# Moving split weights by 64 bytes in SBUF: channel-major pieces at one offset, three placements in the wide products

## The chip, the core and the metric

The kernel runs on one core of a Trainium2 chip. The metric is the device time of one launch in microseconds (us); the time quoted is the median over several runs. A profile is one execution recorded instruction by instruction.

## What is computed

A two-layer decoder trunk on 256 rows of width 2048. Layer 0 is a Mamba-2 mixer, layer 1 an attention over keys and values that are projected from the output of layer 0. Nearly all the arithmetic is in the big projections:

```
proj = h @ in_w                      # 2048 -> 10304: z, x, B, C, dt
y    = chunked_scan(conv(x), ...) * silu(z);  y = group_rms_norm(y) @ out_w   # 4096 -> 2048
x    = layer_norm(alpha*x + (1+gate)*y)
k, v = split(x @ kv_w)               # 2048 -> 2 x 3072
q, z = split(h @ b_in_w)             # 2048 -> 3072 + 1024
o    = merge(attention(q, k, v)) * silu(z);   x = layer_norm(alpha*x + (1+gate)*(o @ b_out_w))
```

where h is x scaled and shifted by two vectors that are matrix products of a condition vector c (scale, shift and gate of each layer). Inputs, weights and output are float32.

## The kernel before

**Split products.** A float32 operand is written as a high half (rounded to the matmul type fp32r) and a low half (what is left), and a product is the sum of three: high x high, high x low, low x high. Weights come from memory in pieces of 128 x 1024 float32 (512 KB). `load_piece` issues the transfer on SP's queue into one of six `raw` tiles; `split` (L96) makes the halves: ScalarE writes `whi` (L99), VectorE writes `wlo` (L101). `whi` and `wlo` are tiles of 128 x 1024 with four buffers each, in the pool `wp`. Beside them, for the activations, stands the long-lived tile `actT`.

**Four forms of product.** They differ in which operand is loaded into the array (stationary, one weight load for each matmul) and which streams through it (moving):

- `cm_piece` (L150 to L152), channel-major: a 128 x 128 block of `whi` or `wlo` is stationary, 256 columns of activations stream. Three matmuls for each block, 24 for each piece.
- `cm_wide` (L181, L184), channel-major: a block of `whi` is stationary for 512 moving columns (the high and low activations beside each other), then a block of `wlo` for 256 columns (the high activations alone). A group of four matmuls (two L181, two L184) does one step of 128 inputs; a product has 16 groups. It serves the xs projections of layer 0 from the third group on ("xs"), the keys ("k"), the queries ("q") and the gate of layer 1 ("z").
- `tm_mults` (L212 to L214), token-major: a 128 x 128 block of activations is stationary and 512 columns of `whi` or `wlo` stream. It serves z of layer 0, the output projections and the values.
- `dt_piece` (L612 to L614): like `cm_piece`, for the 64 dt columns.

**Order of the work.** The first stage (to about 165 us) has a hand-written list `order` of weight pieces between the 32 transfers of 1 MB that make scale and shift of layer 0; each h step waits for two of those. Then follow, in program order, the groups of the scan with one `bc`, `xs` and `z` product each and the scan's own work between them (to about 490 us), the output projection (to 768 us), keys (to 902 us) and values (to 968 us), queries with attention and the gate of layer 1 (to 1183 us), and the last projection with the layer norm. `upcoming` is a list of the pieces that come next, so that the last piece of one product already splits the first of the next (`begin_next`, `first_or`).

**Places in SBUF.** Pools are laid one behind the other in the order in which they are opened: `cons` (constants; among them `cc`, a 32-column tile `pad` that nothing uses, and `ones`, 128 x 128), `wp`, `act` (`actT`), `sm`, `slots`, and the stage pools. `cc` holds the identity, a triangle, and a mask whose last 128 columns are all ones. `ones` is set by VectorE at the start and used by `warm` (matmuls that do nothing but raise the clock, L435) and by one cumulative sum (L698).

Of the kernel before, what the change touches and what calls it, by code (L numbers as in the profile page):

```python
# [9 lines left out]
F32 = mybir.dt.float32  # L10
# [8 lines left out]
P = 128  # L19
# [30 lines left out]
def trunk(ctx, tc, xT, x, c, par, cst, bias, lnrow, ada, wdt, win, wxs, wout, wk, wv, wbin, wbout, out):  # L50
# [20 lines left out]
    nc.scalar.dma_start(crow, c)  # L71
    cc = cons.tile([P, NCONST], F32, name="cc")

    cons.tile([P, 32], F32, name="pad")

    def pv(name):
        a, b = OFF[name]
        return prm[:, a - NB:b - NB]
# [1 line left out]
    ident = cc[:, CI:CI + 128]  # L80
    tri = cc[:, CT:CT + 128]
    cbmask = cc[:, CM:CM + 384]
    ones = cons.tile([P, P], F32, name="ones")
    V.memset(ones, 1.0)


    def rows(t, b):

# [4 lines left out]
        nc.sync.dma_start(raw, src)  # L93
        return raw

    def split(raw, into=None, after=None):  # L96

        hi, lo = into or [wp.tile([P, 1024], F32R, name=n, bufs=4) for n in ("whi", "wlo")]
        copied.append(S.activation(hi, raw, AF.Copy))  # L99
        with tc.issue_after(after) if after is not None else ExitStack():  # L100
            latest.append(V.tensor_tensor(lo, raw, hi.bitcast(F32), op=ALU.subtract))  # L101
        return hi.rearrange("p (k n) -> p k n", k=2), lo.rearrange("p (k n) -> p k n", k=2)
# [7 lines left out]
            with tc.issue_after(copied[-1].ins), tc.issue_after(latest[-1].ins):  # L110
                owed.pop(0)()

    def first_or(src, q):

        return ready.pop() if ready else split(load_piece(src[q]))

    def begin_next():

        if upcoming:
            src, q = upcoming.pop(0)  # L120
            ready.append(split(load_piece(src[q])))

    def behind_next():

# [15 lines left out]
    def cm_piece(src, q, ps, ahi, alo, k0=0, k1=KT, w=None, after=None, ks=(0, 1)):  # L140


        hi, lo = w or split(load_piece(src[q]), after=after)
        for k in ks:
            kt = 2 * q + k
            for n in range(4):
                o = ps[n // 2][:, n % 2, :]
                c_ = slice(n * P, n * P + P)
                first = kt == k0 and n % 2 == 0
                T.matmul(o, hi[:, k, c_], ahi[:, kt, :], start=first, stop=False, skip_group_check=True)  # L150
                T.matmul(o, hi[:, k, c_], alo[:, kt, :], start=False, stop=False, skip_group_check=True)  # L151
                T.matmul(o, lo[:, k, c_], ahi[:, kt, :], start=False, stop=kt == k1 - 1, skip_group_check=True)  # L152
# [4 lines left out]
    def cm_quad(src, ahi, alo, rate=(0, 1), k0=0):  # L157
        ps = acc_pair()
        for q in range(k0 // 2, KT // 2):
            w = first_or(src, q)  # L160
            if q == KT // 2 - 1:
                begin_next()
            cm_piece(src, q, ps, ahi, alo, k0=k0, w=w)
            background(*rate)
        return ps

    def cm_wide(src, dst, rate=(0, 1), moving=None, later=False):

        both, high = moving or (lambda kt: xp[:, kt], lambda kt: xhi[:, kt, :])
        ps = acc_pair()  # L170
        for q in range(KT // 4):
            w = first_or(src, q)
            if q == 1:
                settle()
            if q == KT // 4 - 1:
                begin_next()
            hi, lo = (t.rearrange("p k n -> p (k n)").rearrange("p (k n) -> p k n", k=4) for t in w)
            for k in range(4):
                kt = 4 * q + k
                for n in range(2):  # L180
                    T.matmul(ps[n], hi[:, k, n * P:n * P + P], both(kt), start=kt == 0, stop=False,  # L181
                             skip_group_check=True)
                for n in range(2):
                    T.matmul(ps[n][:, 0, :], lo[:, k, n * P:n * P + P], high(kt), start=False, stop=kt == KT - 1,  # L184
                             skip_group_check=True)
            background(*rate)
        def put():
            for n in range(2):
                S.activation(dst[:, n, :], ps[n][:, 1, :], AF.Copy)
                V.tensor_tensor(dst[:, n, :], ps[n][:, 0, :], dst[:, n, :], op=ALU.add)  # L190

        if later:
            owed.append(put)
        else:
            with behind_next():
                put()
# [137 lines left out]
    with ExitStack() as cA:  # L334
# [15 lines left out]
        with ExitStack() as cS:  # L350
# [38 lines left out]
            def xs_wide(g):  # L389

                xs[g] = pxs.tile([P, 4, L], F32, name="xs")
                for w in range(2):
                    t = xs[g][:, 2 * w:2 * w + 2, :]
                    cm_wide(wxs[2 * g - 4 + w], t, rate=R, moving=(lambda kt: hp[:, :, kt, :], hh_))
                    for n in range(2):
                        conv(t[:, n, :], 4 * g + 2 * w + n, t[:, n, :])

# [31 lines left out]
            with ExitStack() as c0:  # L429
                pe = c0.enter_context(tc.tile_pool(name="pe", bufs=2))  # L430

                def warm(n, at, after=None):
                    for _ in range(n):
                        with tc.issue_after(after.ins) if after is not None else ExitStack():
                            after = T.matmul(at[:, 0, :P], ones, ones, start=True, stop=True)  # L435
                    return after

                at = mm.tile([P, 2, L], F32, name="acc")
# [111 lines left out]

                def high_half(i):

                    halves[i] = [wp.tile([P, 1024], F32R, name=n, bufs=4) for n in ("whi", "wlo")]
                    copied.append(S.activation(halves[i][0][:, 512:], pieces[i][:, 512:], AF.Copy))

                def low_half(i):
# [47 lines left out]
                def dt_piece(q, raw):  # L604

                    if q == 0:
                        pss["dt"] = mm.tile([P, 2, L], F32, name="acc")[:, 0, :]
                    pd = pss["dt"]
                    hi, lo = (t.rearrange("p k n -> p (k n)").rearrange("p (k n) -> p k n", n=P) for t in split(raw))
                    for k in range(8):  # L610
                        kt = 8 * q + k
                        T.matmul(pd, hi[:, k, :], hhi[:, kt, :], start=kt == 0, stop=False)  # L612
                        T.matmul(pd, hi[:, k, :], hlo[:, kt, :], start=False, stop=False)
                        T.matmul(pd, lo[:, k, :], hhi[:, kt, :], start=False, stop=kt == KT - 1)  # L614
                    if q == 0:
                        return
                    row = pe.tile([64, L], F32, name="dtrow", bufs=1)
                    S.activation(row, pd[:64], AF.Identity, bias=pv("dtb")[:64])
                    pt = mm.tile([P, 2, L], F32, name="acc")[:, 0, :128]
                    for b in range(2):  # L620
                        T.transpose(pt[:, 64 * b:64 * b + 64], row[:, b * P:b * P + P], ident[:64, :64])
                    V.tensor_copy(vv, pt)
# [11 lines left out]
                for i, (k, q, ends) in enumerate(order):  # L634
# [7 lines left out]
                    for j in (i, i + 1):  # L642
                        if j < len(order) and j not in halves and order[j][0] != "dt":
                            with tc.issue_after(highs[j // 2 - 1]) if j in (7, 9) else ExitStack():
                                halves[j] = split(pieces[j], after=dots[0] if j == 5 else None)
                    while ended:
                        put_away(*ended.pop())
                    if k == "dt":
# [134 lines left out]

            def firsts(kind, g):
                if kind == "xs" and g > 1:
                    return [(wxs[2 * g - 4 + w], 0) for w in range(2)]
                src, k0, _ = begun.get((kind, g), (None, 0, None))
                if src is None:
                    src = win[{"bc": g // 2, "xs": 4 + g, "z": 6 + g}[kind]]
                return [(src, k0 // 2)]  # L790

            for g in range(G - 1):
                for kind in ("bc",) * (g % 2) + ("xs", "z"):
# [179 lines left out]
    with ExitStack() as cL:  # L973
# [47 lines left out]
        with tc.issue_after(tile4.ins):  # L1021
            state[0] = 0
            queue(pl, cols1[11:])
            jobs.append(lambda: gate_out(1))
            upcoming.extend((wk[2 * (2 * g + hq) + w], 0) for hq in range(2) for g in range(NG) for w in range(2))
            upcoming.extend((wv[1 + 2 * g], 0) for g in range(NG))
            evict_v(0, 2, tm_chunk(wv[4], hx, lx, rate=R))
            for hq in range(2):
                for g in range(NG):
                    kv[hq, g] = place(3 + 3 * hq + g, [P, 4, L])  # L1030
                    for w in range(2):
                        cm_wide(wk[2 * (2 * g + hq) + w], kv[hq, g][:, 2 * w:2 * w + 2, :], rate=R, later=True)
            for g in range(NG):
                evict_v(1, g, tm_chunk(wv[1 + 2 * g], hx, lx, rate=R))
            drain()
# [37 lines left out]

    def queries(hq):
        qq = [pc2.tile([P, 4, L], F32, name=f"q{g}") for g in range(NG)]
        upcoming.extend([(wbin[2 * (2 * g + hq) + w], 0) for g in range(NG) for w in range(2)][1:])
        for g in range(NG):
            for w in range(2):
                cm_wide(wbin[2 * (2 * g + hq) + w], qq[g][:, 2 * w:2 * w + 2, :], rate=(1, 1),
                        later=(g, w) != (NG - 1, 1))  # L1080
        return qq

# [45 lines left out]
    def z_gate(hq, qq):  # L1128
        for w in range(2):
            c_ = slice(2 * w, 2 * w + 2)  # L1130
            z = qq[1][:, c_, :]
            cm_wide(wbin[2 * (6 + hq) + w], z, rate=(1, 2))
            S.activation(z, z, AF.Silu)
            V.tensor_tensor(z, qq[0][:, c_, :], z, op=ALU.mult)
            gate_end[:] = [split_act(oghi[hq][:, c_, :], oglo[hq][:, c_, :], z).ins]
# [237 lines left out]
```

## Time and profile before

| | |
|---|---|
| median of 3 runs | 1237.56 us (1237.37 to 1238.01) |
| profiled execution: its time, its span | 1238.06 us, 1236.3 us |
| granted TensorE clock | 0.999 |
| busy: PE, weight loads, VectorE, ScalarE | 99%, 85%, 83%, 57% of the span |
| read from memory | 331.58 MB, mean 271 GB/s |

The time of the profiled execution is 1.8 us more than its span, which runs from the first to the last recorded instruction. Matmuls overlap and their ends are modelled, so the cost of a matmul in a stream is the distance from its start to the next one's start, not its length: a row of 0.28 us for one matmul may stand beside a distance of 0.12 us. Where consecutive matmuls of one line are merged into one row, the distance is from the start of that row to the start of the next, divided by the count.

### The profile page before, as it was taken

The page shows a single profiled execution, that of the slowest core. Times are in us where ns is not written, and L with a number is a line of the kernel's source. Part 1 is how long each engine was busy: PE and PEld are TensorE (multiplying, and loading weights), DVE is VectorE, ACT ScalarE, POOL GpSimd, SP SyncE. Part 2 cuts the span into 40 slices and gives each one's busy share as a digit, 9 for nine tenths or more (in the row PEclk, how much of TensorE's full clock was granted, in tenths as well). Part 3 has the DMA queues.
Part 4 walks back from the last instruction along what each step waited for, and adds up shares of the span by engine and source line. Part 5 has one row for each costly group of instructions (what it writes and reads, how often), then busy time and mean ns, then how long its engine had stood idle before and what let it go on. Part 6 is the DMA issues. An engine that isn't in the chain of part 4 may idle for free.

```text
span 1236.3 us, 18840 instructions
## 1 busy us (share of the span) xinstructions
PE 1224.5 (99%) x7132; PEld 1052.1 (85%) x7132; DVE 1027.6 (83%) x1456; ACT 702.8 (57%) x1050; POOL 3.9 (0%) x8
## 2 busy tenths in 40 slices
PE   8999999999999999999999999999999999999998
PEld 7889998898888888888888788888888888888886
DVE  6899986999988989899768678888978866758776
ACT  4555477868597789754335544434445644444551
POOL 0000000000000000000000000000000000000001
PEclk9999999999999999999999999999999999999999
DMA  9999977687666456699988569989997774464673
GB/s 378 423 421 422 421 252 248 230 291 253 215 197 206 169 166 210 205 337 351 365 315 296 194 201 359 363 339 370 381 396 291 230 257 145 122 192 133 205 256 68
DMA packets 81371, 336.05 MB, mean 272 GB/s; under 512 B 9200, under 2 KB 9856, under 8 KB 68480
## 3 DMA queue, kind: packets, MB, share of 16 engines
q1 hardware_dynamic: 80352, 333.46, 74.7%
q0 software_dynamic: 576, 1.05, 0.6%
q8 instruction: 56, 0.92, 0.3%
q10 hardware_dynamic: 352, 0.34, 0.1%
q14 instruction: 35, 0.29, 0.1%
HBM read 331.58 MB, written 3.23 MB: 271 GB/s over the span
## 4 chain that ended last, share of the span: by engine, by line
PE 91%; DMA 4%; DVE 2%; ACT 2%; issue 1%; SPq 0%; ACTq 0%; DVEq 0%
PE acc L181 24%; PE acc L213 13%; PE acc L214 13%; PE acc L212 13%; PE acc L184 12%; DMA raw<-in_win 3%; PE acc L150 3%; PE acc L152 3%; PE acc L151 3%; PE py L771 1%; DVE wlo L101 1%; ACT whi L99 1%; PE acc L981 1%; DMA adab<-in_par 1%; PE po L1112 1%
## 5 line engine op out<-in xcount | busy, mean ns | idle before, releaser
L99 ACT ACTIVATE whi<-raw 128x1024 fp32r<-128x1024 f32 x389 | 408.2, 1058 | 352.6 <-PE acc L214 132.8
L101 DVE TENSOR_TENSOR wlo<-raw,whi 128x1024 fp32r<-128x1024 f32 x389 | 468.9, 1221 | 145.0 <-ACT whi L99 139.0
L181 PE MATMUL acc<-actT,whi 128*128 128x512 f32 x1280 | 405.5, 397 | 0.0
L184 PEld LDWEIGHTS acc<-actT,wlo 128*128 128x128 f32 x1280 | 239.4, 188 | 55.6 <-DVE wlo L101 0.4
L213 PE MATMUL acc<-wlo,actT 128*128 128x512 f32 x656 | 257.3, 392 | 2.0 <-DVE wlo L101 2.0
L212 PE MATMUL acc<-whi,actT 128*128 128x512 f32 x656 | 253.4, 394 | 0.0
L184 PE MATMUL acc<-actT,wlo 128*128 128x256 f32 x1280 | 252.8, 279 | 0.0
L295 DVE SCALAR_TENSOR_TENSOR araw<-araw,cb__72 128x2048 f32<-128x2048 f32 x95 | 217.0, 2284 | 3.7 <-DMA araw<-in_ada 3.5
L181 PEld LDWEIGHTS acc<-actT,whi 128*128 128x128 f32 x1280 | 196.0, 189 | 0.4
L214 PE MATMUL acc<-whi,actT 128*128 128x512 f32 x432 | 169.0, 391 | 0.0
L213 PEld LDWEIGHTS acc<-wlo,actT 128*128 128x128 f32 x656 | 123.2, 188 | 29.0 <-DVE wlo L101 3.9
L212 PEld LDWEIGHTS acc<-whi,actT 128*128 128x128 f32 x656 | 122.7, 188 | 24.6 <-ACT s L632 0.5
L150 PE MATMUL acc<-actT,whi 128*128 128x256 f32 x372 | 104.3, 284 | 1.7 <-ACT actT L499 1.0
L151 PE MATMUL acc<-actT,whi 128*128 128x256 f32 x372 | 104.3, 283 | 0.0
L152 PE MATMUL acc<-actT,wlo 128*128 128x256 f32 x372 | 102.9, 284 | 0.8 <-DVE wlo L101 0.8
L214 PEld LDWEIGHTS acc<-whi,actT 128*128 128x128 f32 x432 | 81.1, 188 | 16.6
L214 PE MATMUL acc<-whi,ylo 128*128 128x512 f32 x224 | 87.5, 391 | 0.0
L150 PEld LDWEIGHTS acc<-actT,whi 128*128 128x128 f32 x372 | 71.0, 192 | 3.0 <-ACT actT L499 1.4
L151 PEld LDWEIGHTS acc<-actT,whi 128*128 128x128 f32 x372 | 71.3, 192 | 0.2
L152 PEld LDWEIGHTS acc<-actT,wlo 128*128 128x128 f32 x372 | 70.1, 192 | 1.4 <-DVE wlo L101 1.4
L214 PEld LDWEIGHTS acc<-whi,ylo 128*128 128x128 f32 x224 | 42.1, 188 | 8.5
L729 ACT ACTIVATE seg<-cbc,cumT 128x128 f32<-128x128 f32 x128 | 41.0, 389 | 5.1 <-DVE wlo L101 2.3
(310 smaller groups left out, 1153.6 us busy)
## 6 DMA issues: line engine op xcount, KB each, us to landing
araw<-in_ada SPq DMA_DIRECT2D x96, 1024.0 KB, 6.9
raw<-in_win SPq DMA_DIRECT2D x109, 512.0 KB, 6.0
raw<-in_wout SPq DMA_DIRECT2D x64, 512.0 KB, 5.5
raw<-in_wbin SPq DMA_DIRECT2D x64, 512.0 KB, 3.8
raw<-in_wxs SPq DMA_DIRECT2D x48, 512.0 KB, 4.5
raw<-in_wv SPq DMA_DIRECT2D x48, 512.0 KB, 6.3
raw<-in_wk SPq DMA_DIRECT2D x48, 512.0 KB, 7.4
cbc<-cumd SPq DMA_DIRECT2D x16, 512.0 KB, 4.9
```

Of the source, the lines that this page charges most:

```text
L99: copied.append(S.activation(hi, raw, AF.Copy))
L101: latest.append(V.tensor_tensor(lo, raw, hi.bitcast(F32), op=ALU.subtract))
L150: T.matmul(o, hi[:, k, c_], ahi[:, kt, :], start=first, stop=False, skip_group_check=True)
L151: T.matmul(o, hi[:, k, c_], alo[:, kt, :], start=False, stop=False, skip_group_check=True)
L152: T.matmul(o, lo[:, k, c_], ahi[:, kt, :], start=False, stop=kt == k1 - 1, skip_group_check=True)
L181: T.matmul(ps[n], hi[:, k, n * P:n * P + P], both(kt), start=kt == 0, stop=False, skip_group_check=True)
L184: T.matmul(ps[n][:, 0, :], lo[:, k, n * P:n * P + P], high(kt), start=False, stop=kt == KT - 1, skip_group_check=True)
L212: T.matmul(o, h_, hi[:, k, :], start=kt == k0, stop=False, skip_group_check=part)
L213: T.matmul(o, h_, lo[:, k, :], start=False, stop=False, skip_group_check=part)
L214: end = T.matmul(o, l_, hi[:, k, :], start=False, stop=kt == k1 - 1, skip_group_check=part)
L295: return V.scalar_tensor_tensor(raw, raw, 1.0, cb_, op0=ALU.mult, op1=ALU.mult, accum_out=mod[layer][:, ct, j:j + 1])
L729: S.activation(seg[:, hh, b, :], cbc[:, hh, b, :], AF.Relu, bias=cumT[:, b, h0 + hh:h0 + hh + 1], scale=-1.0)
```

## The change

`halves_at` makes the two tiles 128 x 1056 instead of 128 x 1024, and hands out 1024 columns of each, beginning at a given column: 0 or 16. Sixteen float32 columns are 64 bytes. `cm_piece`, `cm_quad` and `dt_piece` take both halves at column 16 (`SHORT`). Token-major products take both at column 0 (`LONG`). Wide products have four settings, of (whi, wlo): xs (0, 16), k (16, 16), q (16, 0), z (0, 0). The offset travels with the entries of `upcoming`.

The larger tiles need 8 x 128 = 1024 bytes more in each partition. `pad` (128 bytes) and `ones` (512 bytes) leave `cons`; the cumulative sum takes its ones from the mask in `cc`, and `warm` gets a tile of its own, `full`, in a pool of the first stage, set by VectorE after `magic` and not before it.

```diff
-    cons.tile([P, 32], F32, name="pad")
...
-    ones = cons.tile([P, P], F32, name="ones")
-    V.memset(ones, 1.0)
+    ones = cc[:, CM + 256:CM + 384]
+    SHORT, LONG = (16, 16), (0, 0)
+    WIDE = {"xs": (0, 16), "k": (16, 16), "q": (16, 0), "z": (0, 0)}
...
-    def split(raw, into=None, after=None):
-        hi, lo = into or [wp.tile([P, 1024], F32R, name=n, bufs=4) for n in ("whi", "wlo")]
+    def halves_at(off):
+        return [wp.tile([P, 1056], F32R, name=n, bufs=4)[:, o:o + 1024] for n, o in zip(("whi", "wlo"), off)]
+    def split(raw, into=None, after=None, off=(0, 0)):
+        hi, lo = into or halves_at(off)
...
-        hi, lo = w or split(load_piece(src[q]), after=after)
+        hi, lo = w or split(load_piece(src[q]), after=after, off=SHORT)      # cm_piece
...
-            w = first_or(src, q)
+            w = first_or(src, q, SHORT)                                      # cm_quad
...
-            w = first_or(src, q)
+            w = first_or(src, q, WIDE[kind])                                 # cm_wide
...
+                full = pe.tile([P, P], F32, name="ones", bufs=1)
+                V.memset(full, 1.0)
-                            after = T.matmul(at[:, 0, :P], ones, ones, start=True, stop=True)
+                            after = T.matmul(at[:, 0, :P], full, full, start=True, stop=True)
...
-                                halves[j] = split(pieces[j], after=dots[0] if j == 5 else None)
+                                halves[j] = split(pieces[j], after=dots[0] if j == 5 else None,
+                                                  off=LONG if str(order[j][0])[0] == "z" else SHORT)
```

More of the change, by code (lines that the diff above doesn't have):

```diff
@@ L111, in settle, with first_or @@
                 owed.pop(0)()
-    def first_or(src, q):
-        return ready.pop() if ready else split(load_piece(src[q]))
+    def first_or(src, q, off=(0, 0)):
+        return ready.pop() if ready else split(load_piece(src[q]), off=off)
     def begin_next():
         if upcoming:
-            src, q = upcoming.pop(0)
-            ready.append(split(load_piece(src[q])))
+            src, q, off = upcoming.pop(0)
+            ready.append(split(load_piece(src[q]), off=off))
     def behind_next():
@@ L165, in cm_quad, with cm_wide @@
         return ps
-    def cm_wide(src, dst, rate=(0, 1), moving=None, later=False):
+    def cm_wide(src, dst, kind, rate=(0, 1), moving=None, later=False):
         both, high = moving or (lambda kt: xp[:, kt], lambda kt: xhi[:, kt, :])
@@ L393, in xs_wide @@
                     t = xs[g][:, 2 * w:2 * w + 2, :]
-                    cm_wide(wxs[2 * g - 4 + w], t, rate=R, moving=(lambda kt: hp[:, :, kt, :], hh_))
+                    cm_wide(wxs[2 * g - 4 + w], t, "xs", rate=R, moving=(lambda kt: hp[:, :, kt, :], hh_))
                     for n in range(2):
@@ L551, in high_half @@
                 def high_half(i):
-                    halves[i] = [wp.tile([P, 1024], F32R, name=n, bufs=4) for n in ("whi", "wlo")]
+                    halves[i] = halves_at(SHORT)
                     copied.append(S.activation(halves[i][0][:, 512:], pieces[i][:, 512:], AF.Copy))
@@ L608, in dt_piece @@
                     pd = pss["dt"]
-                    hi, lo = (t.rearrange("p k n -> p (k n)").rearrange("p (k n) -> p k n", n=P) for t in split(raw))
+                    hi, lo = (t.rearrange("p k n -> p (k n)").rearrange("p (k n) -> p k n", n=P) for t in split(raw, off=SHORT))
                     for k in range(8):
@@ L785, in firsts @@
                 if kind == "xs" and g > 1:
-                    return [(wxs[2 * g - 4 + w], 0) for w in range(2)]
+                    return [(wxs[2 * g - 4 + w], 0, WIDE["xs"]) for w in range(2)]
                 src, k0, _ = begun.get((kind, g), (None, 0, None))
@@ L789, in firsts @@
                     src = win[{"bc": g // 2, "xs": 4 + g, "z": 6 + g}[kind]]
-                return [(src, k0 // 2)]
+                return [(src, k0 // 2, LONG if kind == "z" else SHORT)]
             for g in range(G - 1):
@@ L1024, in trunk @@
             jobs.append(lambda: gate_out(1))
-            upcoming.extend((wk[2 * (2 * g + hq) + w], 0) for hq in range(2) for g in range(NG) for w in range(2))
-            upcoming.extend((wv[1 + 2 * g], 0) for g in range(NG))
+            upcoming.extend((wk[2 * (2 * g + hq) + w], 0, WIDE["k"]) for hq in range(2) for g in range(NG) for w in range(2))
+            upcoming.extend((wv[1 + 2 * g], 0, LONG) for g in range(NG))
             evict_v(0, 2, tm_chunk(wv[4], hx, lx, rate=R))
@@ L1031, in trunk @@
                     for w in range(2):
-                        cm_wide(wk[2 * (2 * g + hq) + w], kv[hq, g][:, 2 * w:2 * w + 2, :], rate=R, later=True)
+                        cm_wide(wk[2 * (2 * g + hq) + w], kv[hq, g][:, 2 * w:2 * w + 2, :], "k", rate=R, later=True)
             for g in range(NG):
@@ L1075, in queries @@
         qq = [pc2.tile([P, 4, L], F32, name=f"q{g}") for g in range(NG)]
-        upcoming.extend([(wbin[2 * (2 * g + hq) + w], 0) for g in range(NG) for w in range(2)][1:])
+        upcoming.extend([(wbin[2 * (2 * g + hq) + w], 0, WIDE["q"]) for g in range(NG) for w in range(2)][1:])
         for g in range(NG):
             for w in range(2):
-                cm_wide(wbin[2 * (2 * g + hq) + w], qq[g][:, 2 * w:2 * w + 2, :], rate=(1, 1),
+                cm_wide(wbin[2 * (2 * g + hq) + w], qq[g][:, 2 * w:2 * w + 2, :], "q", rate=(1, 1),
                         later=(g, w) != (NG - 1, 1))
@@ L1131, in z_gate @@
             z = qq[1][:, c_, :]
-            cm_wide(wbin[2 * (6 + hq) + w], z, rate=(1, 2))
+            cm_wide(wbin[2 * (6 + hq) + w], z, "z", rate=(1, 2))
             S.activation(z, z, AF.Silu)
```

## The prediction

> **What bounds the kernel now.** I read the page first, its busy table and its chain of work:
>
> ```profile
> span 1236.3 us, 18840 instructions
> PE 1224.5 (99%) x7132; PEld 1052.1 (85%) x7132; DVE 1027.6 (83%) x1456; ACT 702.8 (57%) x1050; POOL 3.9 (0%) x8
> PE 91%; DMA 4%; DVE 2%; ACT 2%; issue 1%; SPq 0%; ACTq 0%; DVEq 0%
> ```
>
> The chain that sets the end runs over PE for 91% of the span, so what counts is the distance between matmul starts. I took those from the timeline of PE at three places, one for each form of product: channel-major pieces, token-major pieces, wide products.
>
> ```profile
> 140.07 0.28 PE L150 MATMUL acc<-actT,whi 128*128 128x256 f32 x1
> 140.19 0.28 PE L151 MATMUL acc<-actT,whi 128*128 128x256 f32 x1
> 140.31 0.28 PE L152 MATMUL acc<-actT,wlo 128*128 128x256 f32 x1
> ...
> 650.28 0.39 PE L212 MATMUL acc<-whi,actT 128*128 128x512 f32 x1
> 650.51 0.39 PE L213 MATMUL acc<-wlo,actT 128*128 128x512 f32 x1
> 650.73 0.39 PE L214 MATMUL acc<-whi,ylo 128*128 128x512 f32 x1
> 650.96 0.39 PE L212 MATMUL acc<-whi,actT 128*128 128x512 f32 x1
> ...
> 800.43 0.40 PE L184 MATMUL acc<-actT,wlo 128*128 128x256 f32 x2
> 800.66 0.63 PE L181 MATMUL acc<-actT,whi 128*128 128x512 f32 x2
> 801.13 0.39 PE L184 MATMUL acc<-actT,wlo 128*128 128x256 f32 x2
> ```
>
> A channel-major matmul costs 120 ns (140.07 to 140.19), a token-major one about 227 ns (650.28 to 650.96, three of them), a wide group 0.70 us (800.43 to 801.13): 0.23 us for its two short products, 115 ns each, and 0.47 us for its two long ones, 235 ns each. For a floor I looked for matmuls of the same widths in plain float32, in the attention; the chain of waits gives four and eight in one piece:
>
> ```profile
> 1044.74 0.86 PE po L1119 x4
> 1045.61 0.89 PE po L1122 x8
> ```
>
> Four passes of 256 columns take 0.86 us, 215 ns each, and eight of 128 columns 0.89 us, 111 ns each. In passes of plain float32 a column streams at half the rate (128 columns in 111 ns, while 256 columns of fp32r take 115 to 120 ns), so 215 and 111 ns are what 512 and 256 fp32r columns would cost at that overhead. Against these, a channel-major matmul has 9 ns too much, a token-major one 12, a wide long product 20, a wide short one 4. This excess is all that a better place for the weights can win.
>
> The Trainium skill, page "TensorE: Matmul & The Clock Gate", section "Back-to-back issue gap", gives N / 2.4 + 2.5 ns, which is 216 ns for 512 columns; the 215 ns row agrees, the fp32r rows do not, and the sum by it would be the same excess.
>
> **Where a faster matmul would count.** Windows over the stages, then those of L150 alone, which is a third of the channel-major matmuls (L151 and L152 follow it one for one), then the waits of the first stage:
>
> ```profile
> 60.00:110.00 50.00, 49.24 (x263) 42.54 (x263) 47.04 (x50) 28.17 (x37) 0.00 (x0) 1.00 1.02 422
> 110.00:155.00 45.00, 45.00 (x365) 44.47 (x364) 42.27 (x46) 23.22 (x29) 0.00 (x0) 1.00 1.02 421
> 200.00:218.20 18.20, 18.20 (x152) 18.14 (x151) 8.94 (x9) 17.21 (x29) 0.00 (x0) 1.00 0.78 282
> 257.70:280.20 22.50, 22.50 (x132) 19.66 (x131) 22.41 (x38) 16.52 (x26) 0.00 (x0) 1.00 0.75 255
> 286.20:308.80 22.60, 22.60 (x133) 19.74 (x130) 22.60 (x42) 22.21 (x43) 0.00 (x0) 1.00 0.74 263
> 770.00:902.00 132.00, 132.00 (x760) 115.17 (x759) 114.25 (x119) 55.44 (x72) 0.00 (x0) 1.00 0.94 364
> 968.00:1183.00 215.00, 215.00 (x1282) 188.29 (x1281) 150.78 (x238) 105.91 (x160) 0.00 (x0) 1.00 0.59 184
> ...
> 0.00:60.00 60.00, 18.65 (x68) 12.68 (x68) 1.00 0.99 399
> 60.00:170.80 110.80, 49.27 (x176) 33.77 (x176) 1.00 0.98 398
> 170.80:260.00 89.20, 27.18 (x96) 18.41 (x96) 1.00 0.72 253
> 260.00:490.00 230.00, 9.26 (x32) 6.12 (x32) 1.00 0.64 211
> ```
>
> ```profile
> ACT whi L99 <- DMA raw<-in_win: 42.3, 26, 3.5
> DVE wlo L101 <- ACT whi L99: 8.3, 15, 1.0
> ```
>
> The columns after the length are PE, weight loads, VectorE, ScalarE, POOL, granted clock, DMA share and GB/s. To 155 us the transfers run at 421 to 422 GB/s with a share of 1.02, and between 20 and 155 us ScalarE's split waits 26 times, 42.3 us in all, for a piece to land. So the pieces arrive at the pace of memory: there a faster matmul waits for the next split, while a slower one would still cost. Most channel-major matmuls lie there: (68 + 176) x 3 = 732 of 1116. In 200 to 218 us ScalarE is busy 17.21 of 18.20 us, and in the xs products (257.7 and 286.2) VectorE is busy 22.41 of 22.50 and 22.60 of 22.60 us. Only the keys (DMA share 0.94, VectorE 114 of 132 us) and the queries (VectorE 151 of 215 us) leave room on all sides.
>
> **The change part by part.**
>
> *What moves and what does not.* `pad` and `ones` take 640 bytes out ahead of the weight pool, the eight larger tiles put 1024 in: everything behind shifts by 384. All three, and the new tile pitch of 4224 bytes, are multiples of 128. So modulo 128 only the halves given column 16 move, by 64 bytes, relative to `actT`; modulo 256 the four buffers of a half now alternate.
>
> *Instructions.* None is added in the stream: the same splits, loads and matmuls. At the start the ones are set after `magic` and not before:
>
> ```profile
> 0.83 0.17 DVE L84 MEMSET ones<- 128x128 f32 x1 [0.83 <-PEq L1362]
> 0.95 0.06 DVE L247 MEMSET magic<- 128x2 int32 x1
> 1.18 7.44 DMA adab<-in_par
> ```
>
> The two still take 0.23 us together and the first matmul waits for both; behind it the chain runs over a transfer from 1.18 to 8.62 us, which is the cover, so 0. Without it the cost would be under 0.1 us. The cumulative sum's ones come with the same tile as its triangle, already awaited: 0.
>
> *The price of 64 bytes.* No product in this trace has its halves off the old places, so it must be bounded. Upwards the gain ends at the floor: 9 ns for a channel-major matmul, 4 for a wide short one, 20 for a wide long one. The loss is bounded by the nearest difference of weight loads that the trace has:
>
> ```profile
> L181 PEld LDWEIGHTS acc<-actT,whi x1280: 186/188/193, 257.6 to 1182.0; 128*128 128x128 f32 x183
> L150 PEld LDWEIGHTS acc<-actT,whi x372: 186/192/192, 20.5 to 425.8; 128*128 128x128 f32 x186
> L213 PE MATMUL acc<-wlo,actT x656: 387/389/504, 25.2 to 967.3; 128*128 128x512 f32 x164
> ```
>
> A load of `whi` has a median of 188 ns in wide products and 192 ns in channel-major pieces (minimum, median, maximum of a group), so loads do differ by 4 ns with what streams beside them; twice the present excess (9 ns more) is the far end. For a channel-major matmul I take 5 ns of gain, because the nearest row of the same shape, the wide short product, runs at 115 and not 120 ns. For a shifted wide product I take 3 ns, short or long: between nothing and 4 for the short ones; for the long ones the nearest row is the token-major 227 ns, 8 below the 235, of which I take a third, since it has other operands.
>
> *The sum.* Channel-major: before 60 us 0 (the chain is on DMA); 60 to 170.8 us 528 x 5 ns = 2.6 us offered, 0.5 taken, as the pieces land at memory's pace; 170.8 to 260 us 288 x 5 = 1.4, half kept beside ScalarE, 0.7; later 96 x 5 = 0.5. Together 1.7 us. The 48 dt matmuls are in the 0.5. Wide, with 12 products x 16 groups x 2 = 384 long and 384 short for each of xs, k and q: xs, wlo shifted, 384 x 3 = 1.2, half kept beside VectorE, 0.6; k, both shifted, 768 x 3 = 2.3; q, whi shifted, 384 x 3 = 1.2; z unmoved, 0. Together 4.1 us. Token-major products keep column 0: their place modulo 256 alternates, and as L214 with its stationary block in another pool (`ylo`) takes the 0.23 us of L212 (650.73 to 650.96), I take 0; with 656 matmuls in the group of L213 and as many beside it in L212 and L214, each ns would be 2.0 us either way.
>
> 1238.06 - 1.7 - 4.1 = 1232.3 us for the profiled execution; that one lies 0.5 us above the median, so 1231.8 us. At the far end of the gain (9, 4 and 20 ns; same halves kept) it is 0.5 + 1.3 + 0.9 for channel-major and 0.8 + (1.5 + 7.7) + 7.7 for wide, 20 us: 1217. What is late next in the key stage is DMA: 132 us at 0.94 can shrink to 124 us.
>
> **The rivals.**
>
> *Nothing happens.* The excess belongs to fp32r, whatever the address: then all pitches stay and the time is 1237.6 us. For it: the excess is nearly alike in channel-major (9) and token-major (12) streams, though operands change sides, and L214 with `ylo` is like its neighbours. Against: wide short products, with halves at the same places, have 4 and the long ones 20, so the excess depends on what is read together. The Trainium skill, page "SBUF — State Buffer", section "Who interferes with whom", gives PE two independent read ports, one for the moving operand and one for weight loads, and says that PE never waits on anyone; by that rule the change would do nothing. That 120 against 115 ns stand for one shape speaks against taking it whole.
>
> *The shift hurts.* Halves and `actT` now begin at the same phase modulo 128; if that is the good phase, loads at 64 bytes collide with the stream. Place: every shifted matmul, and now the first stage counts in full, because a slower PE falls behind the transfers. Price: 4 ns (192 against 188) x (528 + 288 + 96 channel-major + 1536 wide) = 9.8 us, so 1247.4 us; at 9 ns 22 us, 1259.6. It decides from the point at which a channel-major matmul takes more than 120 ns or a wide group more than 0.70 us. Against it: 120 ns is worse than 115 at the unshifted place. For it: nothing shows that the present phase is a bad one.
>
> **How the numbers follow.** Under 0.2% (2.5 us) this kernel's measurement can't tell a change from none. The forecast has 0.5, its own range 1217 to 1235; nothing happens, or gains and losses of the forms cancel, 0.17, at 1237.6; the shift hurts, 0.33, 1240 to 1260. Faster 0.50, same 0.17, slower 0.33. For 8 in 10, the range leaves out the last part of the gain below 1221 (about 0.07) and the dearer half of the loss above 1249 (about 0.12).
>
> **What would show it.** The step is right if L150 to L152 follow each other at about 115 ns in 140 and 240 us while the first stage still ends at the same time; if the key stage's group falls from 0.70 to about 0.685 us and xs and q by half as much; and if z and the token-major rows keep 0.70 and 227 ns. It is wrong if z's groups change (then it is the place modulo 256 or of `actT`), if q's groups move while xs's do not or the reverse (then only one half counts), or if channel-major pitches rise.

## The result, and the profile after

The changed kernel takes 1246.62 us (1246.03 to 1247.92, 4 runs) against 1237.78 us for the kernel before (4 runs): a ratio of 1.0071, 95% interval 1.0054 to 1.0089. It is slower by 8.8 us; the forecast was 1231.8 us and its range ended at 1249. The head of the page after, with the chain:

```profile
span 1244.5 us, 18840 instructions
PE 1230.0 (99%) x7132; PEld 1051.9 (85%) x7132; DVE 1029.7 (83%) x1456; ACT 703.4 (57%) x1050; POOL 3.9 (0%) x8
PE 85%; DMA 6%; DVE 5%; ACT 2%; issue 1%; ACTq 0%; DVEq 0%
```

Same instructions, 8.2 us more span; PE is still the bound, and more of the chain (DMA 6 and not 4%, VectorE 5 and not 2%) lies in the first stage. Lines of the program have moved by two or more: L152 to L154 are the channel-major matmuls, L183 and L186 the wide ones, L214 to L216 the token-major ones.

Where the time went is read from the first and last start in each stage. The next rows are the matmuls of one line in the output projection, in the keys and in the queries (with the gate of layer 1), before and then after; each row gives the count, the shortest, median and longest duration in ns, and the first and last start:

```profile
L212 PE MATMUL acc<-whi,actT x336: 389/389/497, 488.7 to 767.2; 128*128 128x512 f32 x168
L181 PE MATMUL acc<-actT,whi x384: 389/396/398, 767.9 to 901.2; 128*128 128x512 f32 x192
L181 PE MATMUL acc<-actT,whi x512: 388/396/481, 967.8 to 1182.3; 128*128 128x512 f32 x171
```

```profile
L214 PE MATMUL acc<-whi,actT x336: 389/392/499, 491.5 to 773.4; 128*128 128x512 f32 x168
L183 PE MATMUL acc<-actT,whi x384: 388/392/398, 774.1 to 906.5; 128*128 128x512 f32 x192
L183 PE MATMUL acc<-actT,whi x512: 387/397/483, 973.9 to 1190.2; 128*128 128x512 f32 x171
```

The output projection, whose pieces were not shifted at all, went from 278.5 to 281.9 us (+3.4). The keys went from 133.3 to 132.4 (-0.9), the queries from 214.5 to 216.3 (+1.8). The projection began 2.8 us later than before, and 1.7 us of that are there when the first stage ends, as the first token-major matmul after it shows, before and then after:

```profile
170.75 0.40 PE L212 MATMUL acc<-whi,actT 128*128 128x512 f32 x1
172.43 0.40 PE L214 MATMUL acc<-whi,actT 128*128 128x512 f32 x1
```

So the biggest part of the loss is in products that the prediction had at 0.

The timeline of PE in the middle of that projection shows the loss begin and end at a piece:

```profile
641.68 0.39 PE L214 MATMUL acc<-whi,actT 128*128 128x512 f32 x1
643.08 0.39 PE L214 MATMUL acc<-whi,actT 128*128 128x512 f32 x1
644.48 0.39 PE L214 MATMUL acc<-whi,actT 128*128 128x512 f32 x1
...
645.18 0.39 PE L214 MATMUL acc<-whi,actT 128*128 128x512 f32 x1
646.55 0.39 PE L214 MATMUL acc<-whi,actT 128*128 128x512 f32 x1
647.91 0.39 PE L214 MATMUL acc<-whi,actT 128*128 128x512 f32 x1
```

From one of these rows to the next it is six matmuls. Up to 645.18 six take 1.40 us, 233 ns each; from there 1.37 and 1.36 us, 227.5 ns each. Which buffer each piece got is not in the trace but in the program: put beside the trace in program order, the recorded matmuls before 645.18 read halves that begin 128 bytes from the beginning of the activations modulo 256, those after it at 0. Taken over the whole run in this way (starts of neighbouring fp32r matmuls, or of neighbouring groups in wide products; gaps with a wait left out), the mean distances are:

| form | before: place 0 | after, by place of the halves less place of the activations, modulo 256 bytes |
|---|---|---|
| token-major | 227.5 ns | at 0: 228.2; at 128: 232.7 (half of them each) |
| channel-major | 119.9 | at 64: 115.2; at 192: 116.1 |
| wide group of four, k (both shifted) | 696.6 | at 64: 693.6; at 192: 690.3 |
| xs (wlo shifted) | 696.6 | whi 0, wlo 64: 702.3; 128, 192: 703.5 |
| q (whi shifted) | 696.6 | whi 64, wlo 0: 712; 192, 128: 704 |
| z (not shifted) | 696.6 | at 0: 698; at 128: 701 |

The tile pitch of 4224 bytes is 128 more than a multiple of 256, so half of the buffers stand at 128 whatever the offset. The short rows carry the same thing: channel-major rows in the bc product of the third scan group, nine matmuls from 246.38 to 247.44, 118 ns each and not 120; and in the keys five groups from 819.77 to 823.23, 692 ns each and not 697:

```profile
246.38 0.28 PE L153 MATMUL acc<-actT,whi 128*128 128x256 f32 x1
247.44 0.28 PE L153 MATMUL acc<-actT,whi 128*128 128x256 f32 x1
...
819.77 0.62 PE L183 MATMUL acc<-actT,whi 128*128 128x512 f32 x2
823.23 0.62 PE L183 MATMUL acc<-actT,whi 128*128 128x512 f32 x2
```

The first stage has another loss. These are its windows after, to be laid beside the 421 to 422 GB/s before (the last column):

```profile
25.00:60.00 35.00, 31.76 (x213) 28.94 (x212) 30.23 (x33) 17.14 (x25) 0.00 (x0) 0.95 1.02 414
60.00:110.00 50.00, 49.22 (x264) 41.91 (x263) 46.89 (x52) 27.22 (x35) 0.00 (x0) 1.00 1.02 414
110.00:155.00 45.00, 44.28 (x361) 43.09 (x360) 41.94 (x46) 23.76 (x30) 0.00 (x0) 1.00 1.02 414
```

The engines of the transfers are as busy (1.02) and move 2% less.

### The profile page after: what moved, and what is told of

It reads as the page before. It is cut to its first block, busy times and chain, and to the rows that moved or that the text cites. A ratio compares the mean times of both kernels' runs of the same rounds, so it can differ in the third digit from the quotient of the medians.

```text
span 1244.5 us, 18840 instructions
## 1 busy us (share of the span) xinstructions
PE 1230.0 (99%) x7132; PEld 1051.9 (85%) x7132; DVE 1029.7 (83%) x1456; ACT 703.4 (57%) x1050; POOL 3.9 (0%) x8
## 4 chain that ended last, share of the span: by engine, by line
PE 85%; DMA 6%; DVE 5%; ACT 2%; issue 1%; ACTq 0%; DVEq 0%
PE acc L183 24%; PE acc L215 12%; PE acc L216 12%; PE acc L214 12%; PE acc L186 12%; DMA raw<-in_win 5%; DVE araw L297 3%; DVE wlo L103 2%; PE py L777 1%; PE acc L152 1%; DMA araw<-in_ada 1%; PE acc L154 1%; PE acc L153 1%; ACT whi L101 1%; PE acc L987 1%
## 5 line engine op out<-in xcount | busy, mean ns | idle before, releaser
L183 PE MATMUL acc<-actT,whi 128*128 128x512 f32 x1280 | 405.1, 396 | 0.0
L186 PEld LDWEIGHTS acc<-actT,wlo 128*128 128x128 f32 x1280 | 239.4, 188 | 55.6 <-DVE wlo L103 0.2
L186 PE MATMUL acc<-actT,wlo 128*128 128x256 f32 x1280 | 256.0, 281 | 0.0
L214 PE MATMUL acc<-whi,actT 128*128 128x512 f32 x656 | 254.9, 396 | 0.0
L183 PEld LDWEIGHTS acc<-actT,whi 128*128 128x128 f32 x1280 | 196.0, 188 | 0.4
L216 PE MATMUL acc<-whi,actT 128*128 128x512 f32 x432 | 170.0, 394 | 0.0
L214 PEld LDWEIGHTS acc<-whi,actT 128*128 128x128 f32 x656 | 122.7, 188 | 26.0
L152 PE MATMUL acc<-actT,whi 128*128 128x256 f32 x372 | 103.2, 281 | 2.9 <-ACT s L637 2.3
L154 PE MATMUL acc<-actT,wlo 128*128 128x256 f32 x372 | 102.2, 282 | 1.7 <-DVE wlo L103 1.6
L216 PEld LDWEIGHTS acc<-whi,actT 128*128 128x128 f32 x432 | 81.2, 188 | 17.6
L216 PE MATMUL acc<-whi,ylo 128*128 128x512 f32 x224 | 88.2, 394 | 0.0
L152 PEld LDWEIGHTS acc<-actT,whi 128*128 128x128 f32 x372 | 70.4, 190 | 4.3 <-ACT s L637 2.8
L154 PEld LDWEIGHTS acc<-actT,wlo 128*128 128x128 f32 x372 | 69.6, 190 | 2.7 <-DVE wlo L103 2.7
L216 PEld LDWEIGHTS acc<-whi,ylo 128*128 128x128 f32 x224 | 42.1, 188 | 9.2
```

The lines of the kernel that those rows point to most:

```text
L214: T.matmul(o, h_, hi[:, k, :], start=kt == k0, stop=False, skip_group_check=part)
L216: end = T.matmul(o, l_, hi[:, k, :], start=False, stop=kt == k1 - 1, skip_group_check=part)
```

## The experiments

**The larger tiles alone, and the activations moved instead.** Two theories stood. The place theory: a matmul's distance depends on where the operand that is loaded lies against the one that streams, modulo 256 bytes, and the loss comes from the tile pitch. The shift theory: the 64 bytes are the loss. The first kernel takes the changed one and sets every offset to 0:

```diff
-    SHORT, LONG = (16, 16), (0, 0)
-    WIDE = {"xs": (0, 16), "k": (16, 16), "q": (16, 0), "z": (0, 0)}
+    SHORT, LONG = (0, 0), (0, 0)
+    WIDE = {"xs": (0, 0), "k": (0, 0), "q": (0, 0), "z": (0, 0)}
```

> The changed kernel with every offset at column 0: the tiles keep 1056 columns, so the four buffers of a half still alternate by 128 bytes modulo 256, and nothing moves by 64. Place theory (the distance between matmul starts depends on where the block that is loaded lies against the streaming operand modulo 256 bytes, and 128 is the bad place for token-major products): half of the 1968 token-major matmuls near 232.6 ns and half near 228, +5 us; wide groups at 128 cost 700 and not 697 ns, +1 us; the first stage as in the changed kernel, +1 us; 1244 to 1245 us. Shift theory (the 64 bytes themselves cost the time): all pitches as before, 227, 120 and 697 ns, and 1237.5 to 1239 us.

It took 1246.45 us, ratio 1.0064 (1.0051 to 1.0077): the whole loss of the change with nothing shifted by 64 bytes. Token-major distances were 228.4 at 0 and 232.8 at 128. The shift theory is out; the 64 bytes cost and win about as much in sum. The total is 1.5 us above the upper end of what was expected, about 1 us of it in the first stage, whose end came 1.9 us later (172.70 us). The wide groups of this kernel show more than was expected of them: beside the program, they took 697 to 698 ns with the halves at 0, 256 and 384 bytes from the activations modulo 512, and 704 ns at 128.

The second kernel leaves the weights of the kernel before where they were and moves the activations, and all behind, by 128 bytes:

```diff
     act = ctx.enter_context(tc.tile_pool(name="act", bufs=1))
+    act.tile([P, 32], F32, name="gap")
```

> The kernel before with one unused tile of 128 bytes between the weight pool and actT: weights and raw pieces stay where they were, all activations move by 128 bytes against them. Place theory: all 1968 token-major matmuls at about 232.6 ns, +10 us; wide groups near 700 ns, +2.5 us; channel-major matmuls near 118.4 ns, -0.5 us; in all about 1249 us, more than the changed kernel, without a larger tile or a 64-byte shift. Shift theory: no 64 bytes anywhere, 1237.5 us.

It took 1246.8 us, ratio 1.0070 (1.0057 to 1.0084). Its output projection, and that of the first kernel:

```profile
L213 PE MATMUL acc<-whi,actT x336: 390/393/496, 490.1 to 774.1; 128*128 128x512 f32 x168
```

```profile
L214 PE MATMUL acc<-whi,actT x336: 389/392/497, 491.8 to 773.8; 128*128 128x512 f32 x168
```

284.0 us with all buffers at 128 and 282.0 with half of them, against 278.5 with none. The 1104 recorded token-major matmuls of this stage at 232.6 and not 227.5 ns make +5.6 us; +5.5 were measured. The total came out 2 us under the expectation, since its wide groups took 697 and not 700 ns: here all buffers stand at 384 modulo 512, the place where they took 697 ns in the first kernel too.

**Everything moved together.** The unused tile of 128 bytes in the constants is taken out of the kernel before, so that weights, raw pieces and activations move by 128 as one:

```diff
-    cons.tile([P, 32], F32, name="pad")
```

> The kernel before without the unused 128-byte tile in the constants: everything behind, weights, raw pieces and activations, moves by 128 bytes together. Place theory: no matmul moves against its partner, all pitches stay and the time is 1237.5 us. Absolute theory (a tile must itself begin at a multiple of 256): token-major 232 ns, about 1248 us. If the transfers of the first stage run slower because the raw pieces moved, they show 414 and not 422 GB/s and the time is 1238.6 us.

1240.7 us, ratio 1.0020 (1.0011 to 1.0029). Token-major 227.6, channel-major 119.9, wide group 697 ns: no matmul changed, so it is the relative place that counts. But the first stage ran at 414 GB/s and its end came 2.4 us later (173.11 us), so the time is 2 us over the 1238.6 us that were expected for slower transfers:

```profile
25.00:60.00 35.00, 32.63 (x212) 29.77 (x211) 30.23 (x33) 17.55 (x25) 0.00 (x0) 0.95 1.02 414
60.00:110.00 50.00, 49.25 (x266) 42.36 (x265) 46.88 (x49) 26.83 (x34) 0.00 (x0) 1.00 1.02 414
```

In the kernel with only the activations (and all behind) moved these windows have 422 GB/s, although the targets of the 1 MB transfers, which lie behind `actT`, had moved by 128 there too. So the loss needs something ahead of `actT` to have moved: the raw pieces, the halves, or constants.

**One tile for both halves.** The changed kernel's offsets, in buffers that all begin at the same place modulo 256:

```diff
-        return [wp.tile([P, 1056], F32R, name=n, bufs=4)[:, o:o + 1024] for n, o in zip(("whi", "wlo"), off)]
+        t = wp.tile([P, 2112], F32R, name="whl", bufs=4)
+        at = (off[0], 1024 + off[1]) if off[0] <= off[1] else (1024 + off[0], off[1])
+        return [t[:, o:o + 1024] for o in at]
```

> The changed kernel with all its offsets, but both halves of a piece in one tile of 2112 columns, so that all four buffers begin at the same place modulo 256 bytes; a half is given back when both are read, which adds some waiting. Place theory: token-major products back at 227 ns, -5.7 us, z of layer 1 back at 697 ns; what stays is xs (702 ns) and q (710 ns) at 64 bytes in one half alone, k at 694 and channel-major at 115 ns; about 1240.5 us. Shift theory: 1246.6 us as the change.

1245.27 us, ratio 1.0057 (1.0044 to 1.0069), 5 us more than expected. The distances did what the place theory says: token-major 227.7, channel-major 116.4, k 693.5, xs 702, q 712 ns. But the common tile changed the order in which instructions were put out: more of the scan of one group now stands inside the output projection, and the stages no longer match. The total is therefore no test; the distances are.

**Separate tiles at a pitch of 4352 bytes.** To have clean totals, the tiles were made 128 x 1088 (4352 = 17 x 256) and room was found elsewhere: a second triangle in the constants, the unused tile in `sm`, and `vv` moved to a pool that ends with the scan. The unused tile in `cons` came back, so that the raw pieces begin at a multiple of 256 again.

```diff
-        return [wp.tile([P, 1056], F32R, name=n, bufs=4)[:, o:o + 1024] for n, o in zip(("whi", "wlo"), off)]
+        return [wp.tile([P, 1088], F32R, name=n, bufs=4)[:, o:o + 1024] for n, o in zip(("whi", "wlo"), off)]
```

First with all offsets at 0:

> Separate tiles of 1088 columns, so a pitch of 4352 bytes, a multiple of 256; every offset at column 0; raw pieces at a multiple of 256 again (the room comes from ones, a second triangle, an unused tile and a tile moved to another pool). Place theory: nothing stands against its partner otherwise than in the kernel before, and the first stage is at 422 GB/s: pitches 120, 227 and 697 ns, 1238 us, the same as before, although the tiles are larger than in the change. If larger tiles or a longer way to what lies behind them cost as such: 1244 us or more.

1238.45 us, ratio 1.0004 (0.9995 to 1.0013): no difference from the kernel before. Larger tiles cost nothing as such.

Then with the places that the distances had shown to be best: token-major 0, channel-major 64, wide 192 bytes for both halves:

```diff
+    SHORT, LONG = (16, 16), (0, 0)
+    WIDE = {"xs": (48, 48), "k": (48, 48), "q": (48, 48), "z": (48, 48)}
```

> The same tiles, with token-major pieces at column 0, channel-major pieces at column 16 (64 bytes) and all four wide forms with both halves at column 48 (192 bytes). Place theory: token-major 227 ns; channel-major 115 to 116 ns, -1.5 us outside the first stage; wide groups 690 and not 697 ns, 640 x 6 ns = -4 us; about 1232.5 us, faster than both kernels. Shift theory (64 bytes off costs): over 1240 us.

1233.02 us, ratio 0.9962 (0.9950 to 0.9975), faster than both kernels and 0.5 us from what was expected. Its output projection, keys and queries, from an execution of 1235.28 us, the slowest of the five:

```profile
L215 PE MATMUL acc<-whi,actT x336: 387/389/497, 488.3 to 767.3; 128*128 128x512 f32 x168
L184 PE MATMUL acc<-actT,whi x384: 388/392/394, 767.9 to 899.9; 128*128 128x512 f32 x192
L184 PE MATMUL acc<-actT,whi x512: 387/392/482, 966.5 to 1179.5; 128*128 128x512 f32 x171
```

279.0, 132.0 and 213.0 us against 278.5, 133.3 and 214.5: the token-major stage is as before, the wide ones gain 1.3 and 1.5 us. Wide groups took 690.4 and channel-major matmuls 116.6 ns.

Last, everything at 64 bytes, and everything at 192, token-major pieces too:

> The same tiles, every piece at column 16, token-major ones too. What the token-major form does at 64 bytes is open: at 0 it takes 227.5 and at 128 232.7 ns. If the pitch goes up with the distance from 0, 230 ns and +5 us on it, with wide groups at 693.5 (-2 us) and channel-major as in the change: 1240 us. If 64 is good for every form as it is for the channel-major one, 226 ns, -3 us: 1232 us.

> The same tiles, every piece at column 48 (192 bytes). Token-major open as at 64 bytes: 230 ns or 226 ns; wide groups 690 ns (-4 us), channel-major 116 ns (-1.5 us): 1237.5 us, or 1229.5 us.

1238.06 us, ratio 1.0000 (0.9991 to 1.0009), and 1243.45 us, ratio 1.0042 (1.0028 to 1.0055). The output projections, 64 first:

```profile
L215 PE MATMUL acc<-whi,actT x336: 388/388/501, 488.5 to 768.8; 128*128 128x512 f32 x168
```

```profile
L215 PE MATMUL acc<-whi,actT x336: 390/394/502, 488.6 to 773.8; 128*128 128x512 f32 x168
```

280.3 and 285.2 us: token-major matmuls take 229.2 ns at 64 and 233.3 ns at 192. So 64 is dearer than 0 for them, if little, and 192 is about as bad as 128. At 64 bytes the run lies between the two times expected, nearer to the one for a slower token-major form; at 192 both were too low, since the form is worse there than the 230 ns that were thought of.

**The raw pieces alone.** The kernel before with the six `raw` tiles, and a few small constants ahead of them, moved by 128 bytes (`raw` in a pool of its own, unused tile out of `cons`, a gap behind `raw`), and the same with 64:

```diff
-    cons.tile([P, 32], F32, name="pad")
+    wg.tile([P, 32], F32, name="gap")        # in a pool between the raw pieces and the halves
```

> The kernel before, with only the six raw pieces (and a few small constants ahead of them) moved by 128 bytes; weight halves, activations and everything behind stay at their old bytes. If the transfers are slower because their destination no longer begins at a multiple of 256 bytes: 414 and not 422 GB/s in the first stage, all matmul pitches as before, and 1240 to 1240.7 us, as when everything was moved by 128. If the slower first stage there came from something else that moved (the tiles of the 1 MB transfers, the activations): 422 GB/s and 1238 us.

> The same with 64 bytes in place of 128. If it is the multiple of 256 that counts, as slow as with 128 or slower: 414 GB/s or less and 1240 us or more. If only some places are bad, 422 GB/s and 1238 us.

1239.28 us, ratio 1.0008 (0.9999 to 1.0017), and 1239.86 us, ratio 1.0009 (1.0000 to 1.0018). The windows of the one with 128:

```profile
25.00:60.00 35.00, 31.87 (x216) 28.90 (x215) 30.52 (x35) 16.98 (x25) 0.00 (x0) 1.00 1.02 416
60.00:110.00 50.00, 49.24 (x263) 42.24 (x261) 47.13 (x50) 28.01 (x37) 0.00 (x0) 1.00 1.02 417
```

416 to 417 GB/s (416 and 418 with 64 bytes): half of the drop, which neither expectation had, and 0.8 and 1.4 us in the medians, at the edge of what the intervals show. The raw pieces (or the constants ahead of them) are one part of it; moving the activations and what lies behind them alone had left 422. The drop to 414 was seen in the four kernels where both the raw pieces and the tiles behind them had moved. The packets in the traces say the same: from 25 to 140 us, one of 8 KB (a row of a 1 MB transfer) took 309 ns before, 310 with the activations and all behind moved, 313 with the raw pieces moved, and 316 with both; one of 4 KB (a row of a raw piece) 159.5, 159.5, 161 and 162 ns. Why the other half needs both stays open.

## Why the prediction was wrong

**What bounds the kernel** was right for the stages after the first. For the first, "the pieces arrive at the pace of memory" was only half of it: the chain of the kernel before runs over PE there, from 60.8 to 170.8 us.

```profile
by line: PE acc L152 19.2%; PE acc L151 19.0%; PE acc L150 19.0%; PE acc L213 12.5%; PE acc L214 12.3%; PE acc L212 11.9%; PE acc L613 1.7%; PE acc L612 1.7%; PE acc L614 1.6%; DVE wlo L101 1.1%; ACT whi L99 1.0%; issue 0.1%
```

So matmuls and transfers were nearly even, and whichever gets slower sets the pace. That little was to be gained there was right all the same: at 422 GB/s and with channel-major matmuls at 116 ns, the first token-major matmul behind the stage came at 171.61 us in the kernel with the best places and at 170.12 us in the one with everything at 64 bytes, against 170.75. The excess over the floor was also the right quantity to look at: the rows after show that it depends on the place. The Trainium skill's rule, page "SBUF — State Buffer", section "Who interferes with whom", that PE's two read ports are independent and PE never waits on anyone, would have left all distances alone; the runs differ from it by up to 6 ns for each matmul, at equal instructions.

**The step that failed** is the one that priced the token-major products: "their place modulo 256 alternates, and as L214 with its stationary block in another pool (`ylo`) runs at the pitch of L212, I take 0". The comparison row didn't test what it was used for: `ylo` and `actT` both begin at multiples of 256 in the kernel before, so a place of 128 never occurred there. The price for each ns was nearly right (2.0 us; with those whose activations stand in tiles other than `actT`, there are 2172 matmuls of 512 columns, so 2.2 us). The mean cost was 3 ns (5.2 ns in half of them, 0.8 in the rest), 6.5 us in place of 0.

**The wide products** were mis-sized, for k not by much: 3 ns for each shifted product made -2.3 us, measured -0.9. A gain for one half alone was the wrong sign: xs, taken at -0.6 us, cost 6 ns for each of 192 groups, +1.2 us; q, taken at -1.2, cost 11 ns, +2.2 us. Shifting both halves together wins 3 to 6 ns, shifting one loses 6 to 15. The prediction treated the two halves as independent terms. They follow each other in the stream, and in the profile after a load of `whi` starts at 820.36 us, while the matmuls of `wlo` started at 820.23 and the next ones follow at 820.47; that this is why one half can't be priced alone was not shown.

**Channel-major** was right: 5 ns forecast, 4.7 and 3.8 measured. Behind the first stage that is 384 x 4.2 = 1.6 us; the forecast had 1.2.

**The first stage** was taken at -0.5 us and cost 1.7: the shift by 640 bytes was noted, but only the matmuls were asked about it, not the transfers that write there.

The parts add up: token-major +6.5, xs +1.2, q +2.2, k -0.9, z +0.2, channel-major -1.6, first stage +1.7 make 9.3 us, of which up to 0.7 is counted twice, since one token-major matmul in ten lies in the first stage; 8.2 us were measured between the spans.

**The rivals.** "The shift hurts" named 1247.4 us, 0.8 from the result, but by a mechanism that the runs refute: channel-major distances fell, and the kernel without any 64-byte shift is just as slow. That the number came so near is luck. Of its two signs, a wide group above 0.70 us did come, but for xs and q alone, where one half was shifted. "Nothing happens" is out too, since every form's distance changed. The forecast's own signs spoke early: z's groups rose to 700 ns at 128, which it had put down as the sign of "the place modulo 256 or of `actT`".

## What to carry to other kernels

Before a tile is enlarged by a few bytes, ask what its buffers' pitch is modulo 256, and keep operands that the matmul unit reads together at the same relative place: here 32 more columns in a tile put half of the token-major matmuls 2% further apart (232.7 and not 227.5 ns), and tiles of 64 more columns, at a pitch that is a multiple of 256, cost nothing. When a comparison row is to show that something doesn't matter, check that the thing really differed in that row. What takes room elsewhere (here an unused tile and 512 bytes of ones) moves the targets of transfers too.

## What the runs showed of the hardware

The distance between the starts of fp32r matmuls depends on the place of the weight halves less that of the activations, modulo 256 bytes, and differently for each form:

| form (stationary; moving columns) | 0 | 64 | 128 | 192 |
|---|---|---|---|---|
| token-major (activations; 512 of weights) | 227.5 | 229.2 | 232.6 | 233.3 ns |
| channel-major (weights; 256 of activations) | 119.9 | 115.8 | 119.0 | 117.4 ns |
| wide group (weights, both halves at one place; 2 x 512 and 2 x 256 of activations) | 696.6 | 693.5 | 697 or 704 | 690.4 ns |

Column 0 is from the kernel before, 64 and 192 from the kernels with all pieces there, 128 from the one with the activations moved. For the wide group at 128 the place modulo 512 counts too: in the kernel with the larger tiles alone it took 703.8 ns at 128 and 696.9 at 384, and in the one with the activations moved, where all stand at 384, 697 ns. For the token-major form these two places differ little (232.7 and 233.0 ns). Of the four places tried each form has its own best: 0, 64 and 192. Why a place is good was not shown, only that it is relative. From 25 to 110 us transfers into SBUF ran at 422 GB/s with raw pieces at a multiple of 256 bytes, at 416 to 418 when these (and small constants ahead of them) were moved by 64 or 128, and at 413 to 414 when all behind them moved as well.
